# RWKV-7 layer in a two-layer decoder on one core: the triangles' lower blocks per chunk, a and r without zero halves, key products by heads

## The chip, the cores and the metric

The program runs on one core of one Trainium2 chip. The metric is the device time of one execution in microseconds (us), input in HBM to output in HBM. PE is TensorE (its weight loads are listed as PEld), DVE is VectorE, ACT is ScalarE, POOL is GpSimd, and SP is the queue from which nearly all DMAs are issued.

## The reference

One sequence of 1024 tokens, width 1024, passes two layers. Layer 0 mixes over time with the RWKV-7 recurrence (16 heads of 64), layer 1 with a forgetting attention; each is followed by a mixture of experts (32 experts, two per token). The change is in layer 0's recurrence:

```
def step(state, inp):                       # per head, state 64 x 64
    r_t, w_t, k_t, v_t, a_t, b_t = inp
    sa = einsum('bhij,bhj->bhi', state, a_t)
    state = state * w_t + sa b_t^T + v_t k_t^T
    return state, einsum('bhij,bhj->bhi', state, r_t)
...
y = wkv7_scan(rh, exp(w_log), kh, vh, -kk, kk * ah)
y = ((y - mean) * rsqrt(var + GN_EPS)) * gn_g + gn_b
y = ((y + bonus) * g) @ w_o
x = layer_norm(ALPHA * x + (1 + gt_m) * y)
h = x * (1 + sc_f) + sh_f                   # input of the experts and of their router
```

## The kernel before

**Chunks.** The 1024 steps are taken in 16 chunks `c` of 64 tokens. Inside a chunk the steps are coupled by a unit lower triangle of 64x64 per head; its inverse `TT` lets a whole chunk be done by matmuls. Heads go in pairs `m` (KT = 8): head `e` of a pair lies on partitions 64e to 64e+63. So there are 8 x 16 pairs of triangles. `Inverse` makes the inverses: `spread` brings the triangles `A` into a layout with one triangle per partition, `solve` inverts both 32x32 diagonal blocks of each on DVE and POOL, `blocks` brings them back by PE transposes and two ACT copies per group (one of them masked, L749 and L750), and `merge` (L755 to L776) makes the 32x32 block below the diagonal, two chunks per call: step 0 multiplies with `A`, step 1 with the transposed diagonal block `N`, and the four results of a call are copied into `TT` by DVE and ACT. `keep` stores `TT` to DRAM (`TTd`), from where `load_chunk` fetches each chunk's own.

**The opening.** Ahead of the chunks stand `load_chunk(0)`, `load_chunk(1)`, `prep(0)`, `blocks`, then all eight merges with `prep(1)` among them and four keeps, and `router_weights`. Then the memory of the triangles is freed, and in that memory `weights` begins: the row `gate0` is loaded (L1126), and eight slabs of the output weight (`wor`, two loads of 256 KB each) are loaded, multiplied by it on DVE (L1136), and split into `woh` and `wol`.

**A chunk.** `prep(c+1)` makes what does not depend on the state: `prod`, the key products `pG` (with mask: `GT`) from `BK` (b and k) and `AR` (a and r), the transposes `pbt`, the bonus `pbon`. `AR` holds each head of a pair with zeros in the other head's 64 partitions, so that one 128-row matmul serves a head; ACT writes the zeros once for three buffers (L925). `chain(c)` depends on the state `S`: `prhs` from S and GT, `R` (DVE, L1002), `pu` = TT times R (L1011), its copy into `UV`, `pS` and the new S, `pY`. `Mixer.post(t)` runs for each pair of chunks (a tile of 128 tokens): group norm, `pyt` transposes, `pwo` (output projection, 48 matmuls of 128x512), layer norm, the router's logits `plg` and `router.tile` (`pc`, then a run of small DVE rows that ends in `rso`, then `ptab`). These are generators: after each piece of `chain` one piece of `prep` and of every open side generator is written, and `Order` keeps PE's instructions in that written order. DVE, ACT, POOL and SP have orders of their own, set when the kernel is built; each engine works through its list strictly in order.

```
for c in range(NCH):
    with order:
        if c + 2 < NCH:
            mx.load_chunk(c + 2)
        prep = [mx.prep(c + 1)] if 0 < c < NCH - 1 else []
        for _ in mx.chain(c):
            run_all(prep)
            run_all(side)
        ...
        if c % 2:
            side.append(mx.post(c // 2))
```

Of the kernel before, what the change touches and what calls it, by code (L numbers as in the profile page):

```python
# [679 lines left out]
class Inverse:  # L680
# [59 lines left out]
    def blocks(self):  # L740

        nc, g, X, TT = self.g.nc, self.g, self.X, self.TT
        for i0 in range(0, 32, 4):
# [9 lines left out]
        self.N = self.sp.tile([P, P, 32], F32, name="N", tag="X")

    def merge(self, c0, ps):  # L755

        nc, N, TT = self.g.nc, self.N, self.TT
        A = self.A.rearrange("p (m c) t -> p m c t", m=KT)
        qs = slice(c0 * KT, c0 * KT + 2 * KT)
        with self.g.tc.issue_after(self.last.ins) if c0 else ExitStack():  # L760
            nc.vector.transpose(N[:, qs], TT[:, qs, 0:32])
        for step in range(2):
            p = ps.tile([P, 2 * KT, 32], F32, name="pe", tag="sm")
            for q in range(2 * KT):
                c, m = c0 + q // KT, q % KT
                for e in range(2):
                    lo, hi = slice(e * 64, e * 64 + 32), slice(e * 64 + 32, e * 64 + 64)
                    if step == 0:
                        nc.tensor.matmul(p[lo, q], A[hi, m, c, 0:32], TT[hi, c * KT + m, 32:64], start=True, stop=True,
                                         tile_position=(e * 64 + 32, e * 64))  # L770
# [94 lines left out]
def post_mixer(g, pool, psG, l, t, r, wr, br, xr, tag, router, tags, end=lambda: None):  # L865
# [30 lines left out]
    yield  # L896
    yield
    yield
    yield
    router.tile(t, logit, pool)  # L900


class Mixer:
# [11 lines left out]
    def load_chunk(self, c):  # L915
# [5 lines left out]
        if c < 3:  # L921
            q.AR = sp.tile([P, KT, 2, 2, C], F32, name=f"AR{c}")
            for e in range(2):
# [3 lines left out]
        else:  # L927
            q.AR = self.ch[c - 3].AR
        for i, d in enumerate((g.AHd, g.RTd)):
            for e in range(2):  # L930
                r = slice(e * 64, e * 64 + 64)
                nc.sync.dma_start(q.AR[r, :, e, i], d[:, r, c * C:(c + 1) * C].rearrange("m p t -> p m t"))
        q.TT = sp.tile([P, KT, C], F32, name="TTl", bufs=2)
        if c > 1:
            nc.sync.dma_start(q.TT, g.TTd[:, c * KT:c * KT + KT])

    def prep(self, c):
# [4 lines left out]

        q.UV = sp.tile([P, KT, 2, N], F32, name="UV", bufs=2)
        for e in range(2):
            nc.sync.dma_start(q.UV[e * 64:e * 64 + 64, :, e, :],
                              g.Vd[c * C:(c + 1) * C, :].rearrange("t (m e n) -> t m e n", m=KT, e=2)[:, :, e, :])
# [1527 lines left out]
```

## Time and profile before

| | |
|---|---|
| median of 3 runs | 3112.83 us (3109.08 to 3117.62) |
| the profiled execution | 3115.35 us, span 3113.6 us |
| granted TensorE clock, mean | 0.952 of 2.4 GHz |
| PE busy | 2861.3 us, 92% |
| DVE busy | 2394.0 us, 77% |
| ACT busy | 1700.5 us, 55% |
| POOL busy | 807.0 us, 26% |

All times in views are microseconds from the start of the span. The recurrence lies between about 550 and 1020 us. Busy shares are sums over the whole span; the recurrence has stretches with different limits, so the views below are cut by stretch. PE's matmul records can overlap, so the pace of PE is read from the start of one group to the start of the next.

### The profile page before, as it was taken

Reading aid. Unit: us, or ns where it says so; the run is one execution under the profiler, and the core shown is the slowest. Engines: PE = TensorE matmul, PEld = TensorE weight load, DVE = VectorE, ACT = ScalarE, POOL = GpSimd, SP = SyncE. Lnnn points to the kernel's source line nnn. Section 1 sums busy time; section 2 is a strip of 40 time slices with the busy share of each in tenths; the row PEclk is TensorE's granted clock in tenths of the full one; section 3 lists DMA queues with packets and bytes.
Section 4 is the critical chain, followed back from the end, with each engine's and each line's share of the span. In section 5 each row is a group of like instructions: output and inputs, shape, how many; then the busy total and the mean of one; then the engine's idle time right before and its main releaser. Section 6 shows DMA issues by size and latency. Waiting matters only on the chain. (4 is left out here: it accounts for less than half of the span.)

```text
span 3113.6 us, 51077 instructions
## 1 busy us (share of the span) xinstructions
PE 2861.3 (92%) x19763; PEld 2194.2 (70%) x19763; DVE 2394.0 (77%) x3565; ACT 1700.5 (55%) x2563; POOL 807.0 (26%) x429
## 2 busy tenths in 40 slices
PE   6989998669998899999988999999999799999997
PEld 5658777558786677667757989976668577766773
DVE  7477558477887899999976546238867899999996
ACT  4432554432333777767746324337763477776774
POOL 4010316100000433354420005201113433334440
PEclk9989998669999899999999999999999899999998
DMA  7488573585544899999986755639844499999995
GB/s 210 145 260 264 176 233 127 116 178 128 132 124 150 330 383 388 385 354 350 377 325 196 217 191 185 201 109 215 175 107 174 153 393 387 379 367 348 369 376 227
DMA packets 362034, 771.11 MB, mean 248 GB/s; under 512 B 134723, under 2 KB 236315, under 8 KB 311742
## 3 DMA queue, kind: packets, MB, share of 16 engines
q1 hardware_dynamic: 277596, 630.23, 58.7%
q0 software_dynamic: 29104, 70.55, 7.9%
q10 hardware_dynamic: 55090, 67.04, 6.6%
q8 instruction: 157, 2.57, 0.3%
q14 instruction: 87, 0.71, 0.1%
HBM read 664.06 MB, written 120.18 MB: 252 GB/s over the span
## 5 line engine op out<-in xcount | busy, mean ns | idle before, releaser
L1392 DVE TENSOR_TENSOR mlo<-mraw,mhi 128x1024 fp32r<-128x1024 f32 x752 | 875.6, 1221 | 17.3 <-ACT mhi L1387 16.8
L1387 ACT ACTIVATE mhi<-mraw 128x1024 fp32r<-128x1024 f32 x752 | 749.2, 1052 | 204.0 <-PE pd L1484 96.3
L1364 POOL DMA_INDIRECT Yd<-yo,sidx x64 | 389.1, 6079 | 424.2 <-DVE yo L1512 412.5
L1932 PE MATMUL ptk<-wh,hhi 128*128 128x256 f32 x768 | 214.5, 286 | 8.2 <-ACT ksq L1944 4.5
L1932 PE MATMUL ptk<-wl,hhi 128*128 128x256 f32 x768 | 214.0, 283 | 0.0
L1484 PE MATMUL pg<-mhi,xTl 128*96 128x512 f32 x512 | 205.0, 400 | 4.1 <-DVE xTl L69 4.1
L1484 PE MATMUL pd<-mhi,hTh 128*96 128x512 f32 x512 | 208.3, 407 | 0.0
L1932 PE MATMUL ptk<-wh,hlo 128*128 128x256 f32 x768 | 205.7, 283 | 0.2 <-DVE hlo L69 0.2
L1484 PE MATMUL pg<-mhi,xTh 128*96 128x512 f32 x512 | 204.7, 400 | 0.5 <-ACT xTh L68 0.5
L1484 PE MATMUL pd<-mhi,hTl 128*96 128x512 f32 x512 | 205.1, 401 | 0.0
L1484 PE MATMUL pu<-mhi,xTh 128*96 128x512 f32 x512 | 204.6, 400 | 0.0
L1484 PE MATMUL pd<-mlo,hTh 128*96 128x512 f32 x512 | 203.8, 398 | 0.0
L1484 PE MATMUL pg<-mlo,xTh 128*96 128x512 f32 x512 | 203.5, 397 | 0.0
L1484 PE MATMUL pu<-mhi,xTl 128*96 128x512 f32 x512 | 202.2, 395 | 0.0
L1484 PE MATMUL pu<-mlo,xTh 128*96 128x512 f32 x512 | 201.2, 393 | 0.0
L1932 PEld LDWEIGHTS ptk<-wh,hhi 128*128 128x128 f32 x768 | 145.1, 191 | 13.8 <-ACT ksq L1944 6.4
L1358 POOL DMA_INDIRECT xb<-Hd,gidx x64 | 76.8, 1199 | 288.5 <-PE pxt L1471 284.9
L1932 PEld LDWEIGHTS ptk<-wl,hhi 128*128 128x128 f32 x768 | 146.4, 191 | 0.3 <-issue 0.2
L1932 PEld LDWEIGHTS ptk<-wh,hlo 128*128 128x128 f32 x768 | 141.0, 190 | 2.3 <-issue 1.7
L2196 DVE CUSTOM_DVE_ANT_0 lg<-psc,nf 128x256 f32<-128x256 f32 (+7 forms) x128 | 91.6, 752 | 49.3 <-PE psc L2188 49.3
L1512 DVE SCALAR_TENSOR_TENSOR yo<-pd,gtab,mgt 96x512 f32<-96x512 f32 x128 | 93.2, 743 | 28.9 <-PE pd L1484 28.4
L1484 PEld LDWEIGHTS pg<-mhi,xTl 128*96 128x96 f32 x512 | 83.8, 164 | 42.6 <-DVE xTl L69 6.2
(555 smaller groups left out, 6827.5 us busy)
## 6 DMA issues: line engine op xcount, KB each, us to landing
mraw<-in_moe_wgate_dram SPq DMA_DIRECT2D x128, 1024.0 KB
mraw<-in_moe_wup_dram SPq DMA_DIRECT2D x128, 1024.0 KB
mraw<-in_moe_wdown_dram SPq DMA_DIRECT2D x128, 1024.0 KB
adaw<-in_ada_w_dram SPq DMA_DIRECT2D x48, 512.0 KB
mraw<-in_ada_w_dram SPq DMA_DIRECT2D x32, 512.0 KB
Q<-Qd POOLq DMA_DIRECT2D x64, 256.0 KB
adk<-in_ada_w_dram SPq DMA_DIRECT2D x16, 512.0 KB
adaw<-in_kv_ada_w_dram SPq DMA_DIRECT2D x16, 512.0 KB
```

Of the source, the lines that this page charges most:

```text
L1358: return g.nc.gpsimd.indirect_dma_start(out=X[0:SL], out_offset=None, in_=g.Hd[l][:, :], in_offset=bass.IndirectOffsetOnAxis(ap=idx[0:SL], ...
L1364: return g.nc.gpsimd.indirect_dma_start(out=g.Yd[l][:, :], out_offset=bass.IndirectOffsetOnAxis(ap=idx[0:SL], axis=0), in_=Yo[0:SL], in_of ...
L1387: self.ex.g.nc.scalar.activation(hi, raw, AF.Copy)
L1392: self.ex.g.nc.vector.tensor_tensor(lo, raw, hi.bitcast(F32), op=ALU.subtract)
L1484: self.g.nc.tensor.matmul(p, a[:, k, :], b[:, kk, s], start=(k == 0 and j == 0), stop=(k == n - 1 and j == len(tt) - 1))
L1512: self.g.nc.vector.scalar_tensor_tensor(yo[0:SL, s], p, gcol[0:SL], self.gt[0:SL, s], op0=ALU.mult, op1=ALU.mult)
L1932: nc.tensor.matmul(p[:, 0:KU], x[:, t * P:(t + 1) * P], w[:, k, :], start=(k == 0 and j == 0), stop=(k == KT - 1 and j == 2))
L2196: self.g.nc.vector.tensor_tensor_reduce(lg[:, 0:u.W].rearrange("p (s w) -> p s w", s=u.ns), u.sc[e][:, 0:u.ns, 0:u.w], self.k[u.m][1][e][: ...
```

## The change

- **Lower blocks.** `merge` makes those of chunks 0 and 1 only. `TT` of chunks 2 to 15 is stored without them, by two keeps of 1.8 MB each, right behind `blocks`. Each later `prep(c)` makes its own with `lower`, called twice (with `AL`, the part of A needed, loaded from DRAM, and with `iv`, a DVE transpose); its results are copied by ACT. `store` saves the two last `m` of A, which had not been in DRAM.
- **a and r.** `AR` has no zeros: half the size, two loads rather than four per chunk, no fills on ACT. The products with S go to the 64x64 tile of a head (they were 128 rows by 64).
- **Key products.** Eight matmuls of 128x128x256 per chunk become sixteen of 64x128x128, one per head, the two heads of a pair into two PSUM banks.
- **pY.** All products with S first, then those with GT.
- **Copies.** The masked copy in `blocks` goes from ACT to DVE.
- **Order.** `prep(1)` moves into `chain(0)`; `router_weights` moves from ahead of the chunks into `weights`, behind the eighth slab; `xr` has two buffers and `nT`, `hrow` have their own; the router waits two pieces ahead of `pc` and two ahead of `ptab` (before: four ahead of `router.tile`), and `post_mixer` has one piece more.

```
+    def store(self, m0, m1):
+        self.g.nc.sync.dma_start(self.g.Ad[:, m0 * NCH:m1 * NCH], self.A[:, m0 * NCH:m1 * NCH])
...
-            nc.scalar.activation(by(slice(i0, i0 + 4)), src, AF.Copy, scale=g.blk0)
+            nc.vector.tensor_scalar(by(slice(i0, i0 + 4)), src, g.blk0, None, op0=ALU.mult)
...
+    def merge(self, ps):
+        nc, TT = self.g.nc, self.TT
+        N = self.sp.tile([P, 2 * KT, 32], F32, name="N", tag="X")
+        nc.vector.transpose(N, TT[:, 0:2 * KT, 0:32])
+        A = self.A.rearrange("p (m c) t -> p c m t", m=KT)
         for step in range(2):
...
+            for c in range(2):
+                s = slice(c * KT, c * KT + KT)
+                self.last = lower(self.g, ps, TT[:, s], N[:, s] if step else A[:, c], step)
...
+def lower(g, ps, TT, w, step):
+    nc = g.nc
+    p = ps.tile([P, KT, 32], F32, name="pe", tag="sm")
+    for m in range(KT):
+        for e in range(2):
+            o = e * 64 + 32 * (step == 0)
+            nc.tensor.matmul(p[e * 64:e * 64 + 32, m], w[o:o + 32, m, 0:32], TT[o:o + 32, m, 32:64], start=True, stop=True,
+                             tile_position=(o, e * 64))
+    for e in range(2):
+        r = slice(e * 64, e * 64 + 32)
+        last = nc.scalar.copy(TT[r, :, 32:64], p[r])
+    return last
...
+    yield from router.tile(t, logit, pool)
...
-        if c < 3:
-            q.AR = sp.tile([P, KT, 2, 2, C], F32, name=f"AR{c}")
-            for e in range(2):
-                r = slice(64 - e * 64, 128 - e * 64)
-                nc.scalar.activation(q.AR[r, :, e].rearrange("p k i t -> p k (i t)"), g.ones[r, None, :].to_broadcast([64, KT, P]),
-                                     AF.Copy, scale=0.0)
-        else:
-            q.AR = self.ch[c - 3].AR
+        q.AR = sp.tile([P, KT, 2, C], F32, name="AR", bufs=3)
         for i, d in enumerate((g.AHd, g.RTd)):
-            for e in range(2):
-                r = slice(e * 64, e * 64 + 64)
-                nc.sync.dma_start(q.AR[r, :, e, i], d[:, r, c * C:(c + 1) * C].rearrange("m p t -> p m t"))
+            nc.sync.dma_start(q.AR[:, :, i], d[:, :, c * C:(c + 1) * C].rearrange("m p t -> p m t"))
         q.TT = sp.tile([P, KT, C], F32, name="TTl", bufs=2)
         if c > 1:
             nc.sync.dma_start(q.TT, g.TTd[:, c * KT:c * KT + KT])
+            q.AL = sp.tile([P, KT, 32], F32, name="AL", bufs=2)
+            nc.sync.dma_start(q.AL, g.Ad.rearrange("p (m c) t -> p c m t", m=KT)[:, c, :, 0:32])
+        else:
+            self.load_uv(c)
...
-            nc.vector.tensor_tensor(prod[r], q.AR[r, :, e, 1], q.BK[r, :, e, :], op=ALU.mult)
+            nc.vector.tensor_tensor(prod[r], q.AR[r, :, 1], q.BK[r, :, e, :], op=ALU.mult)
+        if c > 1:
+            iv = sp.tile([P, KT, 32], F32, name="iv")
+            nc.vector.transpose(iv, q.TT[:, :, 0:32])
+            lower(g, ps.sm, q.TT, q.AL, 0)
...
-        for i2 in range(4):
-            p = ps.sm.tile([P, 2, 2, 2, C], F32, name="pG", tag="sm")
-            for i in range(2):
-                m = i2 * 2 + i
-                nc.tensor.matmul(p[:, i], q.BK[:, m].rearrange("p b t -> p (b t)"), q.AR[:, m], start=True, stop=True)
-            nc.vector.tensor_tensor(q.GT[:, i2 * 2:i2 * 2 + 2], p, g.gmask[:, None].to_broadcast([P, 2, 2, 2, C]), op=ALU.mult)
-            if i2 % 2:
-                p = ps.sm.tile([P, 4, P], F32, name="pbt", tag="sm")
-                for i in range(4):
-                    nc.tensor.transpose(p[:, i, :], q.BK[:, i2 * 2 - 2 + i].rearrange("p b t -> p (b t)"), g.ident)
-                nc.scalar.activation(q.BT[:, i2 * 2 - 2:i2 * 2 + 2, :], p, AF.Copy)
+        for i4 in range(2):
+            ms = slice(i4 * 4, i4 * 4 + 4)
+            p = [ps.sm.tile([P, 4, 2, C], F32, name="pG", tag="sm") for e in range(2)]
+            for i in range(4):
+                for e in range(2):
+                    r = slice(e * 64, e * 64 + 64)
+                    nc.tensor.matmul(p[e][:, i], q.BK[r, i4 * 4 + i].rearrange("p b t -> p (b t)"), q.AR[r, i4 * 4 + i],
+                                     start=True, stop=True)
+            for e in range(2):
+                nc.vector.tensor_tensor(q.GT[:, ms, e], p[e], g.gmask[:, None, e].to_broadcast([P, 4, 2, C]), op=ALU.mult)
+            yield
+            p = ps.sm.tile([P, 4, P], F32, name="pbt", tag="sm")
+            for i in range(4):
+                nc.tensor.transpose(p[:, i, :], q.BK[:, i4 * 4 + i].rearrange("p b t -> p (b t)"), g.ident)
+            nc.scalar.activation(q.BT[:, ms, :], p, AF.Copy)
+            if c > 1 and i4 == 0:
+                lower(g, ps.sm, q.TT, iv, 1)
...
-                                nc.tensor.matmul(pr[r, mi, :], AR[:, m, e, 0], S[:, m, :], start=(mi == 0), stop=False)
+                                nc.tensor.matmul(pr[r, mi, :], AR[r, m, 0], S[r, m, :], start=(mi == 0), stop=False)
...
-            raw = sp.tile([P, D], F32, name="wor", tag=("xr", "y2", "yt")[k % 3], bufs=1 + (OPT["two"] == ("xr", "y2", "yt")[k % 3]))
+            raw = sp.tile([P, D], F32, name="wor", tag=("xr", "y2", "yt")[k % 3], bufs=1 + (k % 3 == 0))
...
+        self.wr, self.br = router_weights(g, self.router.rp, sp, 0, self.ps.sm, "sm", "hrow")
+        yield
...
+            inv.store(KT - 2, KT)
...
+        for c in range(2, NCH, 7):
+            inv.keep(c, c + 7)
...
-        inv.merge(0, ps.sm)
-        for c in range(2):
-            nc.scalar.copy(mx.ch[c].TT, inv.TT[:, c * KT:c * KT + KT])
-        inv.merge(2, ps.sm)
-        inv.keep(2, 4)
-        for _ in mx.prep(1):
-            pass
-        for c in range(4, NCH, 2):
-            inv.merge(c, ps.sm)
-            if c % 4:
-                inv.keep(c - 2, c + 2)
+        inv.merge(ps.sm)
+        for i in range(2):
+            nc.scalar.copy(mx.ch[i].TT, inv.TT[:, i * KT:i * KT + KT])
         with tc.issue_after(inv.last.ins):
             moe_consts(g)
-            mx.wr, mx.br = router_weights(g, rt.rp, mx.sa, 0, ps.sm, "sm", "prod")
...
-                    prep = [mx.prep(c + 1)] if 0 < c < NCH - 1 else []
+                    prep = [mx.prep(c + 1)] if c < NCH - 1 else []
```

In the orders below the new kernel's line numbers are about 13 to 20 higher: L1015 is the row R (L1002 before), L1150 the product wor (L1136), L971 the masked GT (L960), L968 pG (L959), L780 the matmul of `lower`. First DVE where the last slabs of the output weight are multiplied. Of before, the row R is that of chunk 3:

```order
L69 TENSOR_TENSOR wol<-wor,woh 128x1024
L1136 TENSOR_TENSOR wor<-wor,gate_5381 128x1024
L1068 TENSOR_TENSOR yt<-Ye,gmean 128x1024
L1136 TENSOR_TENSOR wor<-wor,gate_5381 128x1024
L960 TENSOR_TENSOR GT<-pG,gmask 128x512
L952 TENSOR_TENSOR prod<-AR_4514,BK_5678 64x512 x2
L69 TENSOR_TENSOR wol<-wor,woh 128x1024
L1002 TENSOR_TENSOR R<-prhs,nrho 128x256
```

Of after, the row R is that of chunk 2:

```order
L957 STREAM_TRANSPOSE iv<-TTl 128x256
L971 TENSOR_TENSOR GT<-pG,gmask 128x4x128
L1150 TENSOR_TENSOR wor<-wor,gate_4819 128x1024
L971 TENSOR_TENSOR GT<-pG,gmask 128x4x128
L69 TENSOR_TENSOR wol<-wor,woh 128x1024
L1079 TENSOR_REDUCE gmean<-Ye 128x16
L1080 TENSOR_SCALAR gmean<-gmean 128x16
L1082 TENSOR_TENSOR yt<-Ye,gmean 128x1024
L954 TENSOR_TENSOR prod<-AR,BK_4954 64x512 x2
L1087 TENSOR_REDUCE gvar<-y_5315 128x16
L826 TENSOR_TENSOR r0tmp<-r0lb,r0sc 128x1024
L1015 TENSOR_TENSOR R<-prhs,nrho 128x256
```

The eighth product wor stood between the R of chunk 2 and that of chunk 3; it now stands ahead of the R of chunk 2, with the first rows of tile 0's group norm (`gmean`, `yt`, `gvar`) and of the layer norm's rows (`r0tmp`) behind it.

Then DVE where the weights begin, of after; the row R is that of chunk 1 (its first half), iv is that of chunk 2:

```order
L1141 TENSOR_SCALAR gate_4819<-gate_4819 128x1024
L957 STREAM_TRANSPOSE iv<-TTl 128x256
L1041 TENSOR_TENSOR S<-pS,Dt 128x256
L971 TENSOR_TENSOR GT<-pG,gmask 128x4x128 x2
L1150 TENSOR_TENSOR wor<-wor,gate_4819 128x1024 x2
L69 TENSOR_TENSOR wol<-wor,woh 128x1024
L1150 TENSOR_TENSOR wor<-wor,gate_4819 128x1024
L69 TENSOR_TENSOR wol<-wor,woh 128x1024
L1150 TENSOR_TENSOR wor<-wor,gate_4819 128x1024
L954 TENSOR_TENSOR prod<-AR,BK_4767 64x512 x2
L69 TENSOR_TENSOR wol<-wor,woh 128x1024
L1015 TENSOR_TENSOR R<-prhs,nrho 128x256
```

Before, both halves of chunk 1's R stood among the copies and transposes of the merges, ahead of the row on the gate:

```order
L761 STREAM_TRANSPOSE N<-xg 128x512
L776 COPY xg<-pe 32x16x32
L1002 TENSOR_TENSOR R<-prhs,nrho 128x256
L776 COPY xg<-pe 32x16x32
L761 STREAM_TRANSPOSE N<-xg 128x512
```

Now chunk 1's R stands behind the gate and four products of the weights, and the transpose `iv` of chunk 2 is new between the gate and the state `S`.

Last, PE in a chunk in the steady part of the recurrence. Before, behind `pu`:

```order
L1011 MATMUL pu<-R,TTl 64x64 x16
L959 MATMUL pG<-AR_4514,BK_6369 128x256 x2
L964 MATMUL pbt<-ident,BK_6369 128x128 x4
L1231 LDWEIGHTS tribf
L1231 MATMUL pc<-rM,tribf 128x32
L1232 LDWEIGHTS onebf
L1232 MATMUL pc<-cum,onebf 128x32
L1257 MATMUL ptab<-rrhs,rso 128x64 x2
L1104 MATMUL pwo<-woh,yh 128x512
```

After, behind `prhs`, and further on behind `pS` of the same chunk:

```order
L780 MATMUL pe<-TTl,AL 32x32 x16
L968 MATMUL pG<-AR,BK_6079 128x128 x8
L1249 LDWEIGHTS tribf
L1249 MATMUL pc<-rM,tribf 128x32
L1250 LDWEIGHTS onebf
L1250 MATMUL pc<-cum,onebf 128x32
L1118 MATMUL pwo<-woh,yh 128x512
```

```order
L1038 MATMUL pS<-UV,BT 64x64 x16
L968 MATMUL pG<-AR,BK_6079 128x128 x8
L1277 MATMUL ptab<-rrhs,rso 128x64 x2
L1053 MATMUL pY<-S,AR 64x64 x16
L1055 MATMUL pY<-UV,GT 64x64 x16
```

The matmuls of `lower` (pe) are new in the chunk; `pG` stands in two groups of eight instead of four of two; `ptab` stood right behind `pc` and now has a good part of a chunk between.

## Rows read from the trace of the kernel before

**Rows 1.** The page's head and its first part: the span, then busy time, share and instructions of each engine.

```profile
span 3113.6 us, 51077 instructions
PE 2861.3 (92%) x19763; PEld 2194.2 (70%) x19763; DVE 2394.0 (77%) x3565; ACT 1700.5 (55%) x2563; POOL 807.0 (26%) x429
```

**Rows 2.** Busy time by stretch of the recurrence: the stretch, its length, then PE, PEld, DVE, ACT, POOL (busy us and instructions), the granted clock of PE, the DMA engines' busy share and GB/s.

```profile
575.00:632.00 57.00, 43.02 (x1234) 37.96 (x1230) 22.67 (x43) 12.96 (x25) 0.00 (x0) 0.65 0.27 90
632.00:688.00 56.00, 41.38 (x546) 34.14 (x546) 39.84 (x53) 18.50 (x31) 0.00 (x0) 0.74 1.03 219
688.00:717.00 29.00, 19.89 (x245) 16.62 (x244) 22.81 (x28) 7.50 (x11) 6.48 (x2) 0.79 0.33 78
736.00:955.00 219.00, 205.62 (x2906) 171.78 (x2905) 176.94 (x374) 74.91 (x145) 2.77 (x5) 1.00 0.47 122
```

**Rows 3.** The timeline of DVE, the first row R of chunks 1, 2, 3, 4, 5 and 15: start, us, engine, line, operation.

```profile
604.44 0.42 DVE L1002 TENSOR_TENSOR R<-prhs,nrho 128x256 f32<-128x256 f32 x1
...
657.19 0.42 DVE L1002 TENSOR_TENSOR R<-prhs,nrho 128x256 f32<-128x256 f32 x1
...
683.14 0.41 DVE L1002 TENSOR_TENSOR R<-prhs,nrho 128x256 f32<-128x256 f32 x1
...
716.73 0.42 DVE L1002 TENSOR_TENSOR R<-prhs,nrho 128x256 f32<-128x256 f32 x1
...
736.44 0.42 DVE L1002 TENSOR_TENSOR R<-prhs,nrho 128x256 f32<-128x256 f32 x1
...
955.24 0.42 DVE L1002 TENSOR_TENSOR R<-prhs,nrho 128x256 f32<-128x256 f32 x1
```

**Rows 4.** The timeline of ACT and PE ahead of chunk 0: the zero fills, the last copy of `blocks`, and the first `pu`.

```profile
550.36 6.40 ACT L925 ACTIVATE AR<-ones 64x1024 f32<-64x1024 f32 x6
...
573.16 1.15 ACT L750 ACTIVATE xg<-pb,blk 128x512 f32<-128x512 f32 x1
...
584.49 0.80 PE L1011 MATMUL pu<-R,TTl 64*64 64x64 f32 x10
```

**Rows 5.** The timeline of SP's queue: the last keep is issued, then the load of the gate, the first DMA into the freed memory.

```profile
628.24 0.33 SPq L780 DMA_DIRECT2D TTd<-xg  x1
...
632.23 0.32 SPq L1126 DMA_DIRECT2D gate<-modr  x1
```

**Rows 6.** The timeline of DVE: an early slab times the gate (in brackets the idle time before it and what ended it), and the eighth.

```profile
641.15 1.23 DVE L1136 TENSOR_TENSOR wor<-wor,gate 128x1024 f32<-128x1024 f32 x1 [4.01 <-DMA wor<-in_rw_wo_dram]
...
678.85 1.22 DVE L1136 TENSOR_TENSOR wor<-wor,gate 128x1024 f32<-128x1024 f32 x1
```

**Rows 7.** The timeline of PE in the steady part (full clock), neighbouring groups, then two groups of the next chunk, then the group that opens the next pair.

```profile
824.10 1.04 PE L877 MATMUL pht<-ident,xr 128*128 128x128 f32 x8
...
825.57 1.15 PE L1011 MATMUL pu<-R,TTl 64*64 64x64 f32 x32 [0.43 <-DVE R L1002]
826.64 1.13 PE L959 MATMUL pG<-AR,BK 128*128 128x256 f32 x4
827.61 0.60 PE L964 MATMUL pbt<-ident,BK 128*128 128x128 f32 x4
828.05 1.88 PE L893 MATMUL plg<-wr,nT 128*128 128x40 f32 x16
829.75 0.42 PE L1094 MATMUL pyt<-ident,yt 128*128 128x128 f32 x2
...
844.31 0.68 PE L997 MATMUL prhs<-UV,GT 64*64 64x64 f32 x16
844.92 0.69 PE L995 MATMUL prhs<-S,AR 128*64 128x64 f32 x16
...
867.93 0.82 PE L877 MATMUL pht<-ident,xr 128*128 128x128 f32 x6
```

**Rows 8.** The timeline of PE in a merge: 64 records of 32x32 and what follows.

```profile
596.31 1.20 PE L769 MATMUL pe<-xg,A 32*32 32x32 f32 x64
...
597.44 0.49 PE L1025 MATMUL pS<-UV,BT 128*64 128x64 f32 x5
```

**Rows 9.** The timeline of PE: the router's two steps.

```profile
852.47 0.18 PE L1232 MATMUL pc<-cum,onebf 128*128 128x32 bf16 x1
...
854.47 0.63 PE L1257 MATMUL ptab<-rrhs,rso 128*128 128x64 f32 x4 [1.82 <-DVE rso L1253]
```

**Rows 10.** Busy time in one pair of chunks, columns as in rows 2.

```profile
823.98:867.93 43.95, 41.48 (x585) 34.62 (x583) 35.70 (x76) 14.98 (x29) 0.53 (x1) 1.00 0.52 134
```

**Rows 11.** Waits of PE: waiting group, what it waited for, then us in all, times, us each; the first two of 540 to 720 us, the others of 720 to 957 us.

```profile
PE pyt L1094 <- issue: 9.1, 1, 9.1
PE pG L959 <- ACT AR L925: 8.8, 1, 8.8
...
PE ptab L1257 <- DVE rso L1253: 9.1, 5, 1.8
PE pu L1011 <- DVE R L1002: 2.2, 5, 0.5
```

**Rows 12.** Groups of DVE between 540 and 1060 us: line, operation, count, then busy us in all and mean ns of one, then idle time before and its releaser.

```profile
L960 DVE TENSOR_TENSOR GT<-pG,gmask 128x512 f32<-128x512 f32 x64 | 43.4, 679 | 6.4 <-PE pG L959 6.3
L761 DVE STREAM_TRANSPOSE N<-xg 128x512 f32<-128x512 f32 x8 | 5.7, 712 | 6.1 <-ACT xg L750 6.0
L952 DVE TENSOR_TENSOR prod<-AR,BK 64x512 f32<-64x512 f32 x32 | 21.9, 683 | 2.3 <-POOL X L737 1.6 <-DMA rcrow<-in_ln_b_dram 0.3
```

More of the change, by code (lines that the diff above doesn't have):

```diff
@@ L749, in blocks @@
             nc.scalar.activation(by(slice(32 + i0, 36 + i0)), src, AF.Copy)
-            nc.scalar.activation(by(slice(i0, i0 + 4)), src, AF.Copy, scale=g.blk0)
+            nc.vector.tensor_scalar(by(slice(i0, i0 + 4)), src, g.blk0, None, op0=ALU.mult)
             yield
[L753 to L761, printed above, removed]
-        for step in range(2):
-            p = ps.tile([P, 2 * KT, 32], F32, name="pe", tag="sm")
-            for q in range(2 * KT):
-                c, m = c0 + q // KT, q % KT
-                for e in range(2):
[L767 to L770, printed above, removed]
-                    else:
-                        nc.tensor.matmul(p[lo, q], N[lo, c * KT + m], TT[lo, c * KT + m, 32:64], start=True, stop=True,
-                                         tile_position=(e * 64, e * 64))
-            for e in range(2):
-                r = slice(e * 64, e * 64 + 32)
-                self.last = (nc.vector.tensor_copy if e else nc.scalar.copy)(TT[r, qs, 32:64], p[r])
+    def merge(self, ps):
[3 more added lines that the diff above has]
+        A = self.A.rearrange("p (m c) t -> p c m t", m=KT)
+        for step in range(2):
+            for c in range(2):
+                s = slice(c * KT, c * KT + KT)
+                self.last = lower(self.g, ps, TT[:, s], N[:, s] if step else A[:, c], step)
     def keep(self, c0, c1):
@@ L895, in post_mixer @@
     nc.vector.tensor_tensor(logit, pl[:, 0:40], br, op=ALU.add)
[L896 to L900, printed above, removed]
+    yield from router.tile(t, logit, pool)
 class Mixer:
@@ L935, in load_chunk, with load_uv @@
             nc.sync.dma_start(q.TT, g.TTd[:, c * KT:c * KT + KT])
+            q.AL = sp.tile([P, KT, 32], F32, name="AL", bufs=2)
+            nc.sync.dma_start(q.AL, g.Ad.rearrange("p (m c) t -> p c m t", m=KT)[:, c, :, 0:32])
+        else:
+            self.load_uv(c)
+    def load_uv(self, c):
+        g, q = self.g, self.ch[c]
+        q.UV = self.sa.tile([P, KT, 2, N], F32, name="UV", bufs=2)
+        for e in range(2):
+            g.nc.sync.dma_start(q.UV[e * 64:e * 64 + 64, :, e, :],
+                                g.Vd[c * C:(c + 1) * C, :].rearrange("t (m e n) -> t m e n", m=KT, e=2)[:, :, e, :])
     def prep(self, c):
@@ L941, in prep @@
         tl, q = self.tiles.setdefault(t, Ctx()), self.ch[c]
[L943 to L946, printed above, removed]
+        if c > 1:
+            self.load_uv(c)
         if cp == 0:
@@ L1033, in chain @@
         pY = ps.y.tile([P, KT, N], F32, name="pY")
-        for m in range(KT):
-            for st in range(2):
+        for st in range(1 - (c > 0), 2):
+            for m in range(KT):
                 for e in range(2):
-                    o = slice(64 - e * 64, 128 - e * 64)
-                    if st == 0 and c > 0:
-                        nc.tensor.matmul(pY[o, m], AR[:, m, e, 1], S[:, m, :], start=True, stop=False)
-                    if st == 1:
-                        nc.tensor.matmul(pY[o, m], GT[:, m, e, 1, :], UV[:, m, e, :], start=(c == 0), stop=True)
+                    r, o = slice(e * 64, e * 64 + 64), slice(64 - e * 64, 128 - e * 64)
+                    if st == 0:
+                        nc.tensor.matmul(pY[o, m], AR[r, m, 1], S[r, m, :], start=(m == 0), stop=False)
+                    else:
+                        nc.tensor.matmul(pY[o, m], GT[:, m, e, 1, :], UV[:, m, e, :], start=(c == 0), stop=(c == 0 or m == KT - 1))
         nc.scalar.activation(tl.Y[:, cp], pY, AF.Copy)
@@ L1058, in post @@
                                       src[t * P + cp * C:t * P + cp * C + C, :].rearrange("t (m e n) -> t m e n", m=KT, e=2)[:, :, e, :])
-        xr = (self.end if t == NT - 1 else sp).tile([P, D], F32, name="xr", bufs=1)
+        xr = (self.end if t == NT - 1 else sp).tile([P, D], F32, name="xr", bufs=1 + (t < NT - 1))
         self.last = nc.sync.dma_start(xr, I["x"][0, rt, :])
@@ L1108, in post @@
             yield
-        yield from post_mixer(g, sp, ps.sm, 0, t, self.rows, self.wr, self.br, xr, "sm", self.router, ("yl", OPT["ht"], "vt"), lambda: self.end if t >= NT - 2 else None)
+        yield from post_mixer(g, sp, ps.sm, 0, t, self.rows, self.wr, self.br, xr, "sm", self.router, ("nT", "hrow", "vt"), lambda: self.end if t >= NT - 2 else None)
     def gn_rows(self):
@@ L1142, in weights @@
             yield
+        self.wr, self.br = router_weights(g, self.router.rp, sp, 0, self.ps.sm, "sm", "hrow")
+        yield
         self.rows = mod_rows(g, sp, 0, 0, dict(sc=M_SCF0, sh=M_SHF0), "r0", "y2")
@@ L1229, in tile @@
         nc.vector.tensor_tensor(self.cum[:, t + 1], self.cum[:, t], M, op=ALU.add)
+        yield
+        yield
         pc = self.psum.tile([P, 512], F32, name="pc", tag=self.tag)
@@ L1254, in tile @@
                                 self.rank[:, :, t:t + 1].to_broadcast([P, 2, P]), op=ALU.is_equal)
+        yield
+        yield
         pt = self.psum.tile([P, 512], F32, name="ptab", tag=self.tag)
```

5 lines of the change are left out of this document (2 added, 3 removed).

## The prediction

> **What bounds the kernel now.** I read the page's busy shares first: PE is busy for 92% of the span, DVE for 77% [rows 1]. These are means, so I cut the recurrence by stretch, which gives two regimes. In the steady part (736 to 955 us) PE is busy 205.6 of 219.0 us at the full granted clock, 2.4 GHz, with DVE at 176.9 and the DMA engines at 0.47 [rows 2]: PE bounds. The row R of DVE, once per chunk half, is the milestone: chunk 5 has it at 736.44, chunk 15 at 955.24, so a pair of chunks takes 43.8 us [rows 3], and one such pair holds 41.48 us of PE work in 43.95 us [rows 10].
>
> The opening is different. From R of chunk 1 (604.44) to that of chunk 4 (716.73) are 112 us for three chunks [rows 3], which at the steady pace would be 66. Up to 632 us PE makes the merges; from 632 to 688 the DMA engines are at 1.03 and DVE waits for weights, with PE at a mean clock of 0.74 [rows 2]. There the last wait that ends is a slab: the gate's load is issued at 632.23, right behind the last keep (628.24) [rows 5], and the eighth slab is multiplied at 678.85 [rows 6], 46.6 us after the gate. The R of chunk 3 (683.14) stands right behind that row, and PE's longest single wait, 9.1 us, follows [rows 11]. So the opening hangs on when the memory of the triangles comes free, not on the chunks.
>
> **The opening after the change.**
> 1. Ahead of chunk 0, PE's pG waits 8.8 us for ACT's fills [rows 11], which take 6.40 us [rows 4]; they go. ACT also loses eight masked copies of about 1.15 us [rows 4]; DVE takes them at about 0.68 us each, the price of a masked 128x512 row out of PSUM [rows 12]. Five of them stand within DVE's solve, so it ends 3.4 us later at most; the last copy of the blocks, 573.16 + 1.15 = 574.3 before, I put at 571 (bounds 566 to 576).
> 2. Six of eight merges (two groups of 64 records each, 1.13 us a group from start to start, 596.31 to 597.44 [rows 8], and the copies between) no longer stand ahead of the keeps. The keeps are issued at 571 rather than up to 628.24. The last one before, 1.05 MB, was followed by the gate 4.0 us later [rows 5]; both new ones hold 3.67 MB, an estimate of 12 us by that ratio with one fixed part. The gate's load then goes out at 583 instead of 632.2: 49 us earlier (bounds 45 to 54).
> 3. From the gate to the eighth slab took 46.6 us. The floor is eight slabs at the 4.0 us that DVE waits for one [rows 6], plus 3 for the gate itself: 35. I take 42, nearer to the measured end, since the DMA engines were saturated and the same bytes still come. The eighth slab: 625 (618 to 630).
> 4. DVE works in order, and the changed order puts the eighth product ahead of R of chunk 2. Behind it come the split, GT, the first rows of the group norm and `r0tmp`: about ten rows of 128x1024 at 1.2 us [rows 6] or of 128x512 at 0.68 [rows 12], and what they wait for; 16 us. So R of chunk 2 comes at 641 (before 657.19). The gain of 49 shrinks to 16 here. R of chunk 1, behind gate and slabs, comes at about 605, no earlier than before.
> 5. From there nothing waits for weights. Chunk 4 to 5 took 19.7 us before [rows 3]; with 20 a chunk, R of chunk 3 is at 661 and that of chunk 4 at 681, against 716.73: **36 us**. If the slabs take 46.6 again and a chunk 22, chunk 4 is at 583 + 46.6 + 16 + 44 = 690, a gain of 27; if the slabs don't hold chunk 2 and chunks run at 20 from 605 on, 665, a gain of 52.
>
> **The steady part, per pair of chunks** (43.8 us, PE-bound, so PE's prices count, read start to start):
> - pG: a group of four records takes 827.61 − 826.64 = 0.97 us [rows 7], eight groups a pair, 7.8. After: four groups of 16 records of 64x128 weights and 128 moving columns. Bounds: a 64x64 record with 64 columns takes (826.64 − 825.57)/32 = 33 ns, less a switch 28 (below); twice that for 128 columns with the two heads side by side gives 16 x 56 ns + 0.17 = 1.07 us, 4.3 a pair, −3.5. Or the loads of 128 weight columns go one after another, as in plg, 16 records in 829.75 − 828.05 = 1.70 us, 106 ns each [rows 7]: 1.87 a group, 7.5 a pair, −0.3. I take −2.5: the form is nearer to the 64-row records.
> - A switch between tile forms: 16 records of prhs take 844.92 − 844.31 = 0.61 us, 32 of pu 1.07 [rows 7]; two equations give 28 ns a record and 0.17 us a switch.
> - prhs: its products with S go to 64x64, so all of a chunk's four groups have one form and three switches fall away: −0.5 a chunk, −1.0 a pair.
> - Lower blocks: two groups of 16 matmuls, 32 records each, half of 1.13 [rows 8] plus the switch back: 0.65 each, **+2.6** a pair. Their copies lie on ACT, busy 75 of 219 us [rows 2]; hidden.
> - pY: one switch more each, +0.3. The three PSUM banks of "sm" are shared and pG takes two at once: +0.6 for stalls.
> - ptab waits 1.8 us for `rso` once a pair [rows 9], 9.1 in the steady part [rows 11]. With a good part of a chunk between pc and ptab that wait goes: −1.7. PE's next wait is then R of DVE, 2.2 us over the steady part now [rows 11].
> - DVE gets two transposes of 128x256, 0.36 each (half of 0.712 [rows 12]): 35.7 + 0.7 = 36.4 of 42 us. It stays below PE, which hides them; without that cover they cost 0.7.
>
> Sum −1.7 a pair. Bounds: −3.7 with pG at −3.5, no PSUM stalls and no switch behind the lower blocks; +2.6 with pG at −0.3, ptab's wait kept and stalls of 1.0. Times five pairs: **−8.5 us** (−18 to +13).
>
> Loads: `AL` is new in each chunk and the inverse is wanted a chunk earlier. The load of chunk c+2 is released by pu of chunk c; it is wanted in the next chunk, about 22 us later. By [rows 5] 1 MB took 4.0 us, and this is 0.26 MB: some 17 us of cover. The tail and layer 1 I leave at nothing (±2).
>
> Sum: 36 + 8.5 = 44.5 us off the profiled execution's 3115.35 gives 3071. Its time lies 2.5 us above the median of the runs shown, from which the same sum gives 3068. I say **3070**.
>
> **A rule that speaks against it.** pG's saving rests on two 64-row weight loads going side by side; the nearest rows allow −3.5 and −0.3. The Trainium skill, page "TensorE: Matmul & The Clock Gate", section "LDWEIGHTS (loading the stationary operand)", has the load's time grow with the columns alone, not the rows, so that 64x128 would cost what 128x128 does. By that the pair would save 2.2 us less than taken, 11 over five pairs. Whether two loads on different rows overlap, no row of this trace shows.
>
> **Rivals.**
> - *Loads by columns* (the serial price of pG): opening as forecast, steady part +2.5 in all: 3115.35 − 36 + 2.5 = 3082. For it: plg's 106 ns. Against: 64x64 records run at 28.
> - *The slabs don't hold chunk 2*: opening gain 52, steady 8.5: 3055. For it: PE and ACT have slack there. Against: DVE's order, which is fixed.
> - *The opening is paid later*: the chunks take their weights' wait elsewhere and the steady part gains nothing; 3106 to 3115, no change by the bound of 0.3% (9.3 us, about what a measurement of this kernel can tell from no change).
> - *Slower: a load per chunk decides.* `iv` and the first `lower` open every prep; `iv` waits in DVE's list for TT, and R, GT and S stand behind it. `AL` comes in pieces of 128 bytes; no row here shows such a load. If TT and AL land late by d in each of chunks 3 to 15, PE loses d every chunk: 13 x d against 36 + 8.5 decides from d = 3.4 us; at 5 us, 3115 − 44.5 + 65 = 3136. For it: PE had only 2.5 us idle in a pair, so each wait shows. Against: 17 us of cover and the DMA engines at 0.47.
>
> **How the numbers follow.** Forecast (3058 to 3078) 0.50; loads by columns or other misjudged prices in the chunk (3078 to 3100) 0.22; slabs don't hold 0.14; no change 0.06; slower 0.08. With both parts at their bounds the gain is 27 − 13 = 14 or 52 + 18 = 70, 3101 or 3045; from the median the latter is 3042. The range that leaves out no more than 2 in 10 runs from there, 3042, to 3100. Faster by over 0.3% are the first three, 0.86; same 0.06; slower 0.08.
>
> **What would show it.** In the changed profile: no ACT fills and no wait of pG for them; gate's load at about 583; the eighth slab near 625 and R of chunk 2 some 16 us later; R of chunk 4 near 681; a pair of chunks near 42.1 us; groups of 16 pG records 1.1 us (or 1.9) from start to start; two groups of pe per chunk at 0.65; no 1.8 us wait of ptab. Wrong would make it: R of chunk 2 not before 655, pairs of 44 us or more, or idle PE ended by DMA into TTl or AL.

## The result and the profile after

The changed kernel is slower: median 3138.71 us (3131.32 to 3144.9, 6 runs) against 3117.14 us (3109.08 to 3119.15, 6 runs); the ratio is 1.0074, 95% interval 1.0054 to 1.0093. The forecast was 3070. The page of the changed kernel:

```profile
span 3133.0 us, 51596 instructions
PE 2855.3 (91%) x20019; PEld 2194.4 (70%) x20019; DVE 2400.6 (77%) x3564; ACT 1701.2 (54%) x2597; POOL 856.6 (27%) x429
```

PE does 6 us less work than in [rows 1] in a span 19.4 us longer. The milestone R on DVE, chunks 1 to 5 and 15 (a row of x2 holds both halves), against [rows 3]:

```profile
609.49 0.42 DVE L1015 TENSOR_TENSOR R<-prhs,nrho 128x256 f32<-128x256 f32 x1
642.14 0.42 DVE L1015 TENSOR_TENSOR R<-prhs,nrho 128x256 f32<-128x256 f32 x1
673.59 0.75 DVE L1015 TENSOR_TENSOR R<-prhs,nrho 128x256 f32<-128x256 f32 x2
692.77 0.75 DVE L1015 TENSOR_TENSOR R<-prhs,nrho 128x256 f32<-128x256 f32 x2
717.40 0.75 DVE L1015 TENSOR_TENSOR R<-prhs,nrho 128x256 f32<-128x256 f32 x2
961.56 0.42 DVE L1015 TENSOR_TENSOR R<-prhs,nrho 128x256 f32<-128x256 f32 x1
```

Chunk 4 is reached 24.0 us earlier. Then it is lost: from chunk 4 to 15 the kernel takes 268.8 us (before 238.5), +30.3. From R of chunk 15 to the first `pxt` of the experts 70.3 (67.2), +3.1; from there to the second layer's first `pxt` 1455.6 (1444.3), +11.3; the rest −1.4. Together +19.4. A pair of chunks takes 48.8 us, from 717.40 to 961.56 in five pairs, against 43.8.

Busy time by stretch, columns as in [rows 2]; the last two are 10 us each of one pair:

```profile
575.00:632.00 57.00, 31.49 (x592) 27.97 (x592) 29.97 (x38) 17.92 (x34) 0.00 (x0) 0.67 0.88 248
632.00:688.00 56.00, 40.06 (x702) 35.52 (x703) 36.43 (x56) 17.24 (x33) 6.48 (x2) 0.73 0.48 101
717.00:938.00 221.00, 197.64 (x3206) 169.26 (x3207) 162.91 (x351) 77.38 (x165) 2.78 (x5) 0.90 0.47 118
750.00:760.00 10.00, 6.37 (x130) 5.34 (x130) 4.61 (x13) 1.35 (x2) 0.00 (x0) 0.97 0.62 138
760.00:770.00 10.00, 10.00 (x176) 9.36 (x175) 8.68 (x10) 3.38 (x10) 0.00 (x0) 0.52 0.49 134
```

In the steady part the granted clock was 1.00 before [rows 2] and is 0.90. It falls to its lower level, 1.2 GHz, once per pair: PE idles for 3.6 of the 10 us up to 760, and the 10 us after are granted 0.52. What PE waits for, two pairs later: DVE, SP's queue (with two of its waits between 717 and 938 us: us in all, times, longest), and PE in the same stretch:

```profile
845.47 1.22 DVE L1098 TENSOR_TENSOR yt<-yt,vt 128x1024 f32<-128x1024 f32 x1
...
847.87 0.42 DVE L1271 TENSOR_TENSOR rso<-ramp,rank 128x256 f32<-128x256 f32 x1
854.00 0.45 DVE L957 STREAM_TRANSPOSE iv<-TTl 128x256 f32<-128x256 f32 x1 [5.72 <-DMA TTl<-TTd]
...
857.17 0.67 DVE L971 TENSOR_TENSOR GT<-pG,gmask 128x512 f32<-128x512 f32 x1
```

```profile
846.72 2.54 SPq L1071 DMA_DIRECT2D vt<-Vd  x4
849.35 1.25 SPq L1071 DMA_DIRECT2D gtl<-Gd  x2
850.72 0.55 SPq L928 DMA_DIRECT2D TTl<-TTd  x1
...
SPq L928 <- PE pu L1024: 18.1, 5, 4.8
SPq L1071 <- DVE yt L1098: 14.2, 3, 5.1
```

```profile
844.93 1.15 PE L1024 MATMUL pu<-R,TTl 64*64 64x64 f32 x32
...
851.27 1.16 PE L968 MATMUL pG<-AR,BK 64*128 64x128 f32 x16
852.36 0.66 PE L1277 MATMUL ptab<-rrhs,rso 128*128 128x64 f32 x4
...
857.90 0.78 PE L975 MATMUL pbt<-ident,BK 128*128 128x128 f32 x4 [2.71 <-DVE GT L971]
```

Read from the top: the new tile's `vt` may be loaded only when the old one has been added to `yt` (846.69), and its issue heads SP's queue until then; six loads later TT of the chunk after next is issued (850.72) and lands at 854. DVE's list has `iv` of that chunk ahead of this chunk's S and the next one's GT, so DVE stands for 5.72 us, GT comes late, PSUM stays full, and PE's pbt waits. The buffer itself was free when pu ended (846.08), only 2.2 us before DVE stood at `iv` (848.29).

In layer 1, the small rows of the router lie otherwise. First PE before, then PE, DVE and POOL after:

```profile
2443.21 1.09 PE L877 MATMUL pht<-ident,xr 128*128 128x128 f32 x8 [1.05 <-ACT xr L805]
...
2451.24 0.21 PE L1231 MATMUL pc<-rM,tribf 128*128 128x32 bf16 x1 [2.98 <-DVE rM L1228]
...
2455.20 0.21 PE L1231 MATMUL pc<-rM,tribf 128*128 128x32 bf16 x1 [1.35 <-DVE rM L1228]
```

```profile
2453.73 0.63 PE L1277 MATMUL ptab<-rrhs,rso 128*128 128x64 f32 x4 [0.57 <-DVE brs L808]
2466.41 0.21 PE L1249 MATMUL pc<-rM,tribf 128*128 128x32 bf16 x1 [12.05 <-DVE rM L1244]
...
2466.51 1.94 PE L883 MATMUL pht<-ident,xr 128*128 128x128 f32 x8
...
2458.91 2.27 DVE L1218 CAST tfg<-tig 128x2 f32<-128x2 uint32 x1
2462.23 2.30 DVE L1230 TENSOR_SCALAR rgh<-ramp,tfg 128x4 f32<-128x4 f32 x1
...
2457.20 3.95 POOL L893 TENSOR_TENSOR x<-xr,r1lg 128x1024 f32<-128x1024 f32 x1 [1.42 <-ACT xr L810]
2461.70 2.80 POOL L894 TENSOR_TENSOR x<-x,r1lb 128x1024 f32<-128x1024 f32 x1
```

The routers of the last two tiles were together at the end before, and the last tile's pht stood ahead of both `pc`. Now the `pc` of the last tile but one stands behind a whole chain of DVE rows (12.05 us), and the last tile's pht behind that `pc`, though POOL had the same tile's `xr` at 2457.20. Single small rows in the chain take 2.3 us rather than 0.2 while POOL multiplies, but such rows are not what changed. From 2330 us to the second experts' first `pxt`, 8 rows of at most 256 values per partition take over 1.6 us before and 6 now, each under a row of POOL. Two of before:

```profile
2445.01 2.27 DVE L1202 CAST tfe<-tie 128x2 f32<-128x2 uint32 x1
...
2448.40 2.29 DVE L1222 SCALAR_TENSOR_TENSOR eid<-tfg,tfe 128x2 f32<-128x2 f32 x1
```

### The profile page after: what moved, and what is told of

Same layout as the page of the kernel before. It is cut to its first block, busy times and chain, and to the rows that moved or that the text cites. A ratio compares the mean times of both kernels' runs of the same rounds, so it can differ in the third digit from the quotient of the medians.

```text
span 3133.0 us, 51596 instructions
## 1 busy us (share of the span) xinstructions
PE 2855.3 (91%) x20019; PEld 2194.4 (70%) x20019; DVE 2400.6 (77%) x3564; ACT 1701.2 (54%) x2597; POOL 856.6 (27%) x429
## 5 line engine op out<-in xcount | busy, mean ns | idle before, releaser
L1384 POOL DMA_INDIRECT Yd<-yo,sidx x64 | 422.1, 6595 | 416.2 <-DVE yo L1532 398.5
L1378 POOL DMA_INDIRECT xb<-Hd,gidx x64 | 90.5, 1413 | 247.8 <-PE pxt L1491 235.9
```

The costliest lines, as they stand in the source:

```text
L1378: return g.nc.gpsimd.indirect_dma_start(out=X[0:SL], out_offset=None, in_=g.Hd[l][:, :], in_offset=bass.IndirectOffsetOnAxis(ap=idx[0:SL], ...
L1384: return g.nc.gpsimd.indirect_dma_start(out=g.Yd[l][:, :], out_offset=bass.IndirectOffsetOnAxis(ap=idx[0:SL], axis=0), in_=Yo[0:SL], in_of ...
```

## The experiments

"Pair" is a fifth of the time from R of chunk 5 to R of chunk 15; "clock" is the granted clock from 717 to 938 us, both from one profiled execution of each kernel. Medians are compared with the kernel before, run on the same chips (3113.5 to 3116.5).

**TT's load from ACT's queue.**

```
-            nc.sync.dma_start(q.TT, g.TTd[:, c * KT:c * KT + KT])
+            nc.scalar.dma_start(q.TT, g.TTd[:, c * KT:c * KT + KT])
```

> The changed kernel, with each chunk's load of TT issued from ACT's queue (behind pu's first copies) rather than from SP's, where it stands behind post's vt loads. Theory Q (SP's queue makes TT late, iv waits for it in DVE's list, and the PE idle of 2.7 to 3.6 us that follows once a pair brings the granted clock down): DVE's 5.7 us wait of iv once a pair is gone, PE's wait of pbt for GT (11.2 us in the steady part) falls under 3, the granted clock of the steady part goes from 0.91 to 0.98 or more, a pair from 48.8 to 41 to 43 us, the whole to 3095 to 3112. Rival M (the clock falls because the chunk's matmuls are now smaller): iv's wait goes but the clock stays near 0.91, a pair 45 to 47, the whole 3120 to 3130. Rival P (pbt waits since pG takes two of three PSUM banks): the wait of pbt stays, a pair 47 or more, the whole 3130 to 3140.

3114.85 us, ratio 0.9999 (0.9982 to 1.0016): 24 us back. PE's wait of pbt for GT fell from 11.2 to 1.0 us between 717 and 963. But `iv` still waits (21.8 us between 717 and 938, 31.4 in the changed kernel), the clock is 0.94 there and a pair 46.7, short of the 0.98 and the 41 to 43 us expected. Where pu ended at 742.41 and the load went out at 744.48, `iv` still waited 3.36 us: it stands too early in DVE's list for any issue. Rival P is out; M is not.

**iv behind R.**

```
+            with g.tc.issue_after(self.R.ins):
                 nc.vector.transpose(iv, q.TT[:, :, 0:32])
```

> The changed kernel, with the transpose iv told to stand behind the R of the chunk before in DVE's list; TT's load stays on SP's queue. Theory Q: S and GT no longer stand behind iv's wait, PE's idle once a pair goes, clock 0.98 or more, a pair 41 to 44 us, the whole 3095 to 3115. If TT's landing itself is what PE needs (the first lower of a chunk), a wait of pe for TTl takes its place and the whole stays at 3125 or more.

3113.22 us, ratio 0.9996 (0.9985 to 1.0007), and no wait of iv is left. A pair takes 44.9; the one pair without a fall of the clock 43.5 (R of chunk 8 to that of chunk 10). Its windows, PE's longest wait between 717 and 938 us, and then 10 us each from the wait of chunks 7, 9 and 11 on:

```profile
717.00:938.00 221.00, 206.89 (x3610) 176.62 (x3603) 179.74 (x378) 85.55 (x178) 2.77 (x5) 0.95 0.51 122
...
782.70:826.20 43.50, 40.48 (x748) 34.52 (x746) 36.83 (x78) 17.38 (x37) 0.53 (x1) 1.00 0.61 141
...
PE pu L1025 <- DVE R L1016: 7.7, 8, 1.2
...
757.00:767.00 10.00, 8.41 (x116) 7.43 (x116) 6.50 (x10) 5.69 (x12) 0.01 (x1) 0.66 0.38 101
803.00:813.00 10.00, 8.40 (x142) 7.12 (x142) 8.48 (x15) 6.07 (x12) 0.53 (x1) 1.00 0.47 145
847.00:857.00 10.00, 9.21 (x126) 8.03 (x126) 6.34 (x10) 6.50 (x12) 0.53 (x1) 0.66 0.34 93
```

So where TT was late in two lists at once, mending either recovers the same 24 us, but not the forecast gain. PE's work in an undisturbed pair is 40.48 us, 1.0 less than in [rows 10]; what is left is a longer wait of pu for R (1.15 and 0.79 us, before about 0.5) and a clock of 0.95. The wait is the same in all three chunks; behind that at 803 the clock stays at 1.00, behind the other two it falls.

**More work in the gap.** In the changed kernel, pY twice in even chunks:

```
+        for st in (range(1 - (c > 0), 2) if c % 2 or c == 0 else (0, 1, 0, 1)):
```

> The changed kernel, with the matmuls of pY done twice in even chunks (the same result; 64 records, 2.16 us of PE work more in each of 7 chunks, placed right ahead of the long wait). If it is the length of PE's idle that brings the clock down: the idle shrinks from 2.7-3.6 to 0.5-1.5 us, the granted clock of the steady part rises to 0.97 or more, and the kernel gets faster by 15 to 25 us (3113 to 3124) though PE does 15 us more. If the clock falls for another reason: no change to 8 us slower (3138 to 3147).

A miss: 3160.24 us, ratio 1.0143 (1.0123 to 1.0164). The wait of pbt fell to 1.4 us at most, but a wait of pG for `yl` of up to 3.0 took its place, and the clock stayed at 0.91. This edit doesn't mend DVE's list, it only moves the idle time.

**Router of layer 1 as before.**

```
+    for _ in range(4 * l):
+        yield
     yield from router.tile(t, logit, pool)
...
+        if self.tag == "sm":
+            yield
+            yield
```

> The changed kernel, with the router's pieces in layer 1 as before (four ahead of the router, none inside); layer 0 as changed. The theory that the split router costs layer 1 some 9 us (a wait of pc for rM of 12 us, small DVE rows of 2 us): from 2330 us to the start of the second experts' matmuls layer 1 takes what it took before (9 us less), the whole 3128 to 3131. Rival: the 9 us are the clock's or a load's, and the whole stays within 3 us of 3138.

3128.85 us, 9.9 less than the changed kernel. From the first to the second experts' `pxt` it takes 1443.1 us, as before (1444.3; changed 1455.6). The 11 us of layer 1 are the router's pieces. Seven small rows take over 1.6 us here, so it isn't their number. The profile is of an execution of 3139.47 us: layer 0, left as in the changed kernel, took 15 us more in it up to the first `pxt`, with a clock of 0.86 and a pair of 51.5. So much can lie between two profiles of the same recurrence.

**Lower blocks all ahead** (the change without its first part):

```
+        inv.merge(0, ps.sm)
...
+        for c in range(4, NCH, 2):
+            inv.merge(c, ps.sm)
+            if c % 4:
+                inv.keep(c - 2, c + 2)
```

> The changed kernel without its first part: the lower blocks of all chunks are made ahead of the chunks by merge, as before, and prep has no lower and no iv; everything else as changed. It prices the first part. The gate's load comes at about 625 again and R of chunk 4 at 705 to 715 (before: 716.7, changed: 692.8), so the opening's gain of 24 us belongs to the lower blocks. In the steady part nothing waits for TT: a pair takes 41 to 42 us if the clock holds; if the smaller products alone bring the clock down, it shows 0.97 or less and a pair takes 43 to 45. The whole 3105 to 3120.

3114.65 us, ratio 0.9998. R of chunk 4 at 712.7, a pair 41.7 at a clock of 0.96, with waits of pu for R of up to 2.4 us:

```profile
717.00:938.00 221.00, 204.93 (x3297) 176.79 (x3295) 190.74 (x391) 78.12 (x154) 2.78 (x5) 0.96 0.54 133
PE pu L1019 <- DVE R L1010: 12.3, 9, 2.4
```

So the first part is worth 20 us in the opening (692.8) and costs 7 us a pair as it was built; the other parts save 2.1 a pair.

**Old products** on top of iv behind R. 

> The kernel of the run with the later iv, with the products in their form of before (AR with zero halves, pG as 128x128x256, the products with S from 128 rows, pY in its order of before); the lower blocks are made per chunk. Theory M (the granted clock falls in the stretch of about 20 us per pair in which PE has only matmuls of small tiles and no pwo): the clock of the steady part is 0.99 or 1.00, and a pair takes 44 to 46 us with 4 us more of PE work than the run with the later iv at its full clock (43.5). If the matmuls of lower or the wait for R bring the clock down, it stays at 0.95 or less and a pair takes 47 or more.

3118.25 us; clock 0.95, a pair 49.0. Rival M as I put it is out: with the wide products in place the clock falls all the same, behind waits of up to 1.5 us (plg for GT) in the stretch without pwo. At the same clock of 0.95 a pair is 4.1 us longer than with the new products (44.9). In this kernel DVE's list has R of chunk 2 (619.68) ahead of the last two slabs, and R of chunk 4 comes at 680.68, 36 us earlier than before: so that order held chunk 2 in the changed kernel, as forecast. How much of the 12 us against it (692.77) is the order's own isn't separated, since the products differ too.

**Six wide matmuls more**, and as their control **32 small records more**, both on top of iv behind R, both ahead of (or in) pY of even chunks from 6 on:

```
+        if c > 5 and c % 2 == 0:
+            for i in range(6):
+                nc.tensor.matmul(pY..., self.woh[:, i, 0:P], self.wol[:, i, 0:512], start=True, stop=True)
```

```
+        for j, st in enumerate(range(1 - (c > 0), 2) if c < 6 or c % 2 else (0, 0, 1)):
```

> The kernel of the run with the later iv, with six matmuls of 128x128 by 512 columns more, whose result is overwritten, ahead of pY in the even chunks from 6 on: inside the stretch without pwo, 1.4 us of PE work more in a pair. Theory M: the granted clock of the steady part goes from 0.95 to 0.98 or more, and a pair is no longer than without them (44.9 us). If the clock falls for another reason, it stays and a pair takes 46 to 47.

> The kernel of the run with the later iv, with the matmuls of pY from S done twice in even chunks from 6 on (32 records of 64x64, 1.08 us, the result unchanged): the control to the six wide matmuls, which also gave DVE 1.4 us more ahead of R. If it was the shorter wait for R that held the clock there: the waits of pu for R fall (10 to 3-5 us in the steady part), the clock goes to 0.98, a pair 44 to 44.5. If the width of the matmuls held it: the waits fall as well, but the clock stays at 0.95 or less, and a pair takes 45 to 46.

3104.02 us (0.9971, 0.9959 to 0.9984) and 3109.0 us (0.9979, 0.9965 to 0.9993): with more work on PE, both are faster than the same kernel without it (3113.22). The window of the wide one with its wait for R, then those of the small one:

```profile
717.00:938.00 221.00, 211.37 (x3661) 178.86 (x3661) 182.82 (x388) 85.43 (x182) 2.67 (x5) 0.98 0.52 124
PE pu L1025 <- DVE R L1016: 3.3, 6, 0.8
```

```profile
717.00:938.00 221.00, 209.88 (x3830) 179.58 (x3828) 183.25 (x383) 87.03 (x182) 3.27 (x6) 0.98 0.50 124
PE pu L1025 <- DVE R L1016: 5.2, 9, 0.8
```

The width of the matmuls makes no difference to the clock; in both the longest wait for R is 0.8 us instead of 1.2. PE's delay gave DVE the time to make R. These two runs don't tell the shorter wait from the added work itself as what holds the clock.

**pwo spread over a pair**, on top of iv behind R. 

> The kernel of the run with the later iv, with the four pieces of pwo spread over a pair (two in each chunk, no stretch of 20 us without them) by pauses between them; the two extra pauses ahead of pht are left out. Theory M: the clock of the steady part is 0.98 or more, a pair takes 42 to 43.5 us, the whole 3100 to 3108. If the clock falls for another reason: 0.95, a pair near 45, the whole 3110 to 3117.

A miss: 3146.76 us. The pauses put pht and pc where DVE wasn't ready (waits of pht for `yl` up to 2.6 us, of pe for GT 2.5); PE is busy for 188 of 221 us, clock 0.90. It doesn't test M.

**R first**: prod and post's first product behind R too, instead of filling PE.

```
+            with g.tc.issue_after(self.R.ins) if c > 1 else ExitStack():
                 nc.vector.tensor_tensor(prod[r], ...
...
+        with g.tc.issue_after(self.R.ins):
             nc.vector.tensor_tensor(v3, v3, tl.bon...
```

> The kernel of the run with the later iv, with two more kinds of DVE rows told to stand behind R: prod, and post's first product (vt times bon). Nothing is left out. If the falls of the clock in the run with the later iv (0.95) come from the waits of pu for R (1.15 and 0.79 us) within the stretch without pwo: those waits fall under 0.6, the clock goes to 0.99 or more, a pair from 44.9 to 41 to 42 us, the whole to 3092 to 3102. If the stretch alone is enough: the waits go, but the clock stays at 0.95, a pair 43 to 44, the whole 3103 to 3110.

3104.13 us, ratio 0.9961 (0.9948 to 0.9974). The waits for R are gone (0.4 in all), the clock is 0.98, a pair 43.0. A wait of pbt for GT is back with 6.8 us in five (2.0 at most), since GT now stands behind R. Without any work more on PE the clock is as high as with it, though neither outcome that I expected came: 0.99 and 41 to 42 us, or 0.95.

**The parts together.** 

> The later iv, the six matmuls more ahead of pY in even chunks, and the router's pieces in layer 1 as before. If the parts add up: 3104 less 10 = 3094 (3089 to 3099).

3095.04 us, ratio 0.9927 (0.9909 to 0.9945).

> The later iv, prod and vt behind R, and the router's pieces in layer 1 as before: 10 us less than the run with R first alone, 3082 to 3092 if the clock holds, 3093 to 3100 if not.

3097.93 us, ratio 0.9936 (0.9916 to 0.9957). The parts roughly add up: 9.0 and 6.2 us less than without the router's pieces, which gave 9.9 alone. The clock is 0.97 and 0.98, as in the runs that they build on. Both beat both kernels; the second does no work twice.

## Why the prediction was wrong

- **Opening, right in its mechanism, 12 us too much in size.** The gate's load went out at 587.2 (forecast 583), the eighth slab was multiplied at 632.2 (625), R of chunk 2 came at 642.1 (641). That last agreement is partly luck: the gate was 4 us late, the slabs took 45.0 us (42), and the rows behind them 9.9 (16). Step 5 failed: "From there nothing waits for weights", 20 us a chunk. Chunk 2 to 3 took 31.5 us. pu waited for R's halves, and prb for `rws`, the router's weights that the change had put there; DVE stood 3.29 us for TT in between. The groups behind ran at the lower clock, pS in 1.98 us rather than 1.15.

```profile
642.61 1.12 PE L1024 MATMUL pu<-R,TTl 64*64 64x64 f32 x16 [4.55 <-DVE R L1015]
647.27 1.12 PE L1024 MATMUL pu<-R,TTl 64*64 64x64 f32 x16 [3.54 <-DVE R L1015]
...
657.49 3.60 PE L865 MATMUL prb<-rws,ones 128*128 128x40 f32 x16 [5.41 <-DVE rws L861]
```

- **PE's prices, right, and pG better than taken.** Start to start at full clock: pG 1.09 to 1.16 us for 16 records (1.07 at the better bound), which is 3.2 to 3.4 us a pair saved and not 2.5; a group of lower 0.63 (0.65, though half of 1.13 and a switch of 0.17 add up to 0.74); 16 records of prhs 0.47 (0.45 by 28 ns a record). The Trainium skill's rule on the page "TensorE: Matmul & The Clock Gate", section "LDWEIGHTS (loading the stationary operand)", would have made pG 1.87 by plg's rows if the loads followed one another; here 1.16. The trace agrees with the rule for one load (median 190 ns before, 188 after, with half the rows), so it is their overlap that saves. The same page of the Trainium skill says under "The mechanism" that loads on another row group are pulled ahead of running matmuls, which agrees with the 1.16.
- **ptab, right; R behind it, mis-sized.** ptab's wait is gone from the steady part. But pu's wait for R, left at 2.2 us over five pairs, grew to 1.9 us a pair with iv behind R, so that even a pair at full clock takes 43.5 us and not 42.1.
- **The loads: the step that failed.** "The load of chunk c+2 is released by pu of chunk c ... some 17 us of cover" took the buffer for the only condition. SP works in order too, and the issue stood behind `vt`, which waits for DVE: 850.72, 4.6 us after pu had freed the buffer. And "it is wanted in the next chunk, about 22 us later" failed by more: DVE's list had `iv` in the same chunk, as the order shown with the change already had it, at 848.29, 2.2 us after pu, while the load takes 3.3 us from issue to landing. There was no cover, whatever the queue: with the load on ACT's, `iv` still waited for it eight times, 1.1 to 4.5 us each. The rival that I gave 0.08 named the right place, `iv` in DVE's list with S and GT behind it; but it asked for d in each chunk and priced d as PE's delay. What came was one long wait a pair, and behind it mostly some 10 us at half the clock. Pairs rose by 5.1 us rather than fell by 1.7.
- **The granted clock had no term.** All was priced at 1.00. Nearly every fall stands behind a wait inside the stretch of some 20 us a pair without pwo: before, with waits of 0.4 to 0.9 us there, no fall [rows 2]; with 2.2 to 3.6 us a clock of 0.90; with 1.15 us 0.95; with 0.8, whether filled by wide or small matmuls, 0.98. But the length of the wait doesn't set the loss: with the lower blocks all ahead, waits of up to 2.4 us go with 0.96, with R first 2.0 us with 0.98, and with iv behind R the same wait is followed by a fall in chunks 7 and 11 and by none in chunk 9. The run with pY twice and that with old products show that the wait ahead of pu is not the only condition. That the long waits cost the clock is shown: with iv behind R they are gone, and it rises to 0.95. What else decides stays open.
- **Layer 1, left at nothing, cost 11 us.** I looked at the router's pieces only where the recurrence hides them. In layer 1 the same edit puts one more `pc`, and the last tile's pht behind it, after a chain of DVE rows, with no cover at the end.

## What to carry to other kernels

A transfer's cover is counted from the place of its issue in the queue, not from the release of its buffer: look at what the issues ahead of it wait for. A new row on an engine that works in order is placed by the list, and a row that waits for a DMA must not stand ahead of the rows that the bound engine needs; telling it to stay behind them gave back 24 us here. Ask of that list when the row comes up, not when its result is needed. And in a stretch at full clock, price a wait with the half clock that may follow it, since here 3.6 us of waiting were followed by 10 us at half speed.
